# Two scan halves and one state step of the mixer, one z tile later in the plan

## The chip, the cores and the metric

The kernel runs on one core of a Trainium2 chip. The core has five engines that work beside each other, each through its own list of instructions in order: TensorE (PE, matmuls into PSUM), VectorE (DVE), ScalarE (ACT), GpSimd (POOL) and SyncE (SP, which only issues transfers). POOL issues transfers too, among them all that add to what is already in the target. An instruction waits on semaphores that other engines or landed transfers raise. The metric is device time in microseconds (us) of one execution.

## The reference

One step of a hybrid decoder trunk, all in fp32, for 512 tokens of a new sequence and 8 single new tokens of running ones (520 columns in all): `h += 0.5 ffn1(norm(h))`, `h += mixer(norm(h))`, `h += 0.5 ffn2(norm(h))`, and a last norm. The change lies in the mixer, whose input projection gives four things: `u_pool` (512 features) for a causal pooling mix, `z` (1024) as a gate, `xbc` (1536) for a convolution of four taps followed by SiLU, and `dt` (16 heads). The convolved `xbc` is split in x (1024 = 16 heads of 64), B and C (2 groups of 128 each), and goes through a scan over 4 chunks of 128 tokens:

```python
Acs = jnp.cumsum(dtc * A.reshape(G, Hg), axis=2)
decay = jnp.exp(jnp.where(mask, seg, -jnp.inf))          # seg = Acs[l] - Acs[s]
scores = jnp.einsum('bclgn,bcsgn->bclsg', Cc, Bc)
y_diag = jnp.einsum('bclsg,bclsgh,bcsgh,bcsghp->bclghp', scores, decay, dtc, xc)
states = jnp.einsum('bclgn,bclgh,bclghp->bcghpn', Bc, decay_end * dtc, xc)
# h <- exp(Acs[-1]) * h + states, chunk after chunk; y_off reads the state before its chunk
y_off = jnp.einsum('bclgn,bcghpn,bclgh->bclghp', Cc, h_prev, jnp.exp(Acs))
y = y_diag + y_off + d_skip * x
```

Then `y * silu(z)` is normed by group, joined with the pooling mix, and multiplied by `w_out`. The new states of pooling, convolution and scan are outputs too. The 8 sample tokens take one step of the same recurrence from a given state.

## The kernel before

Activations lie with features on the 128 partitions and the 520 columns along the free axis, in two halves of 260. An fp32 product is made of three matmuls (`mm3`, L122): weights and activations are split in a high and a low part (`whi`, `wlo`, `xh`, `xl`), and hi·hi (L123), hi·lo (L126) and lo·hi (L127) add up in one PSUM bank. A weight tile arrives in `raw` by SP (L119), ACT casts the high part (L107), and for the late kind ACT writes `-raw` rounded (L110) and a transfer of POOL adds the weights to it (L111), which leaves the low part.

The mixer is written as short stages, each named by a letter and a number, and two strings give their order: `CONV_PLAN`, then, after the pool `cv` of the convolution's buffers is released and `cz` is opened, `GATE_PLAN`. The letters that matter here:

- `x j`: input projection of x tile j (48 matmuls), its convolution (`U` emptied from PSUM by L781 to L783, first tap on ACT at L867, three taps on VectorE at L869) and SiLU into `X[:, j]` (L871, L872). `x7` is the last of them.
- `X1`: `sample_x(1)`, one VectorE command (`sxdt`, L965), which reads the sample columns of X tiles 4 to 7.
- `A j`: `ssd_a`, the part of the scan without the state; j runs over chunk j % 4 of group j // 4, so `A3` is the fourth chunk of group 0 and `A4` the first chunk of group 1, which reads X tiles 4 to 7. On PE two small products into `pb` (L1038, L1039) and four transpositions of X into `px` (L1046). A broadcast load fetches the decay rows `ab` from DRAM (L1048, SP). POOL, ACT and VectorE make from them `we` (L1052, L1053), `E` (L1058), `cd` (L1060) and the masked decay in `ab` itself (L1063 to L1068, L1074); from `px` come `xdt` (L1070) and `xw` (L1073), from `pb` come `bt` (L1041) and `scm` (L1043).
- `B j`: `ssd_b`, the step with the state: `yo` (L1083), `pst` (L1086), `yd` (L1089) on PE, the state `hst` (L1095 on POOL, L1096 on VectorE), and the sum into X (L1099 to L1103).
- `z j`: input projection of gate tile j (48 matmuls), emptied into `zs` by L1113.
- `s2`: two sample steps: loads of `cb` (L970) and `h` (L972) on SP, and four VectorE commands each (`junk`, L975).
- `p`, `c`, `m`: the pooling mix; `m j` is six matmuls into `pm`, emptied by L924 and L925. `e0` stores four small states (L1172 to L1175).

The strings are the order in which the program is written down. The builder then moves instructions between engines' lists by its own timeline, and chooses PSUM banks (eight, `ppm`) and buffers, so that a token's instructions may stand some places from where its neighbours are. The buffers that tie the stages are few: `ab`, `bt`, `scm` have three each, `xdt`, `xw`, `we`, `cd`, `E` have two, `cb` shares three with other small tiles, and `h0` has four. A load of `ab` can go out only when the `B` three steps earlier has read its buffer. SP issues in its list's order, so a load also stands behind every transfer ahead of it whose data isn't ready.

Of the kernel before, what the change touches and what calls it, by code (L numbers as in the profile page):

```python
# [36 lines left out]

CONV_PLAN = (
    "b0 b1 d0 b2 b3 x0 x1 v0 d1 x2 x3 d2 X0 p0 y0 c0 A0 p1 x4 m0 x5 B0 c1 p2 m1 A1 x6 c2 p3 A2 B1 x7 "
    "c3 X1 m2 A3 B2 e0"  # L40
)
GATE_PLAN = (
    "A4 z0 s2 B3 z1 s2 m3 z2 s2 B4 z3 s2 A5 z4 s2 B5 A6 z5 G0 s2 z6 A7 s2 z7 s2 B6 o0 H0 o1 B7 o2 G1 "
    "o3 g0 g1 H1 g2 g3"
)
LAST_PLAN = "h0 h2 h1 n0 h3 n1 n2 n3"
# [1252 lines left out]
```

## Time and profile before

| | us |
|---|---|
| median of 3 runs | 981.19 (973.34 to 981.55) |
| profiled execution, own time | 977.54 |
| its span, first to last instruction | 975.8 |
| PE busy | 945.4 |
| VectorE busy | 856.6 |
| ACT busy | 700.3 |
| POOL busy | 233.6 |

The profile is of one execution. Its times count from the first instruction, and its span is 1.74 us shorter than the execution's own time. A row of the timeline gives start, length, engine, line, operation, output and inputs, shape, count of merged instructions, and in brackets the idle time of that engine just before it with what ended it. PE's matmuls overlap: a 260-column matmul is listed with 0.28 us, while the next one starts 0.12 us later. So the time of a piece of PE work is read from start to start. The mixer's plan runs from some 357 to 600 us of the span.

### The profile page before, as it was taken

What the parts mean: (1) busy time and instruction counts of PE and PEld (TensorE: products, weight loads), DVE (VectorE), ACT (ScalarE), POOL (GpSimd) and SP (SyncE); (2) the same over time, 40 slices, a digit from 0 to 9 for tenths busy, and PEclk for the clock granted to TensorE, in tenths of its full rate; (3) what the DMA queues carried; (4) which work ended last, traced back from release to release, by engine and by line L of the source; (5) the groups of instructions that cost most, each with busy time, mean ns of one, the idle gap of its engine ahead of it and who ended that gap; (6) DMA issues with size and microseconds to landing.
All of it is one profiled execution on the core that took longest, in us unless ns stands there. A gap on an engine that the chain in (4) does not pass through costs nothing.

```text
span 975.8 us, 20309 instructions
## 1 busy us (share of the span) xinstructions
PE 945.4 (97%) x7636; PEld 924.0 (95%) x7636; DVE 856.6 (88%) x1610; ACT 700.3 (72%) x1287; POOL 233.6 (24%) x341
## 2 busy tenths in 40 slices
PE   7999999999999999999899999999999999999995
PEld 6999999999999999999799999899999999999995
DVE  7999899989989698688879866999989999999876
ACT  8776777777777475686676546678778788887864
POOL 0111211221121000156522111122332333333300
PEclk9999999999999999999999999999999999999998
DMA  7665766576566243264588777467687678777732
GB/s 242 167 154 136 190 149 148 126 184 180 119 152 165 66 150 118 88 205 117 148 232 225 177 173 165 119 146 179 152 220 185 167 174 222 178 159 189 191 90 89
DMA packets 66739, 157.01 MB, mean 161 GB/s; under 512 B 9608, under 2 KB 22856, under 8 KB 66640
## 3 DMA queue, kind: packets, MB, share of 16 engines
q1 hardware_dynamic: 41168, 103.78, 33.5%
q0 software_dynamic: 25472, 51.92, 29.3%
q8 instruction: 60, 0.98, 0.4%
q14 instruction: 39, 0.32, 0.1%
HBM read 148.33 MB, written 7.34 MB: 160 GB/s over the span
## 4 chain that ended last, share of the span: by engine, by line
PE 81%; DVE 7%; ACT 4%; DMA 4%; issue 2%; POOL 1%; SPq 0%; DVEq 0%; ACTq 0%; POOLq 0%
PE A L127 7%; PE A L123 7%; PE A L126 7%; PE BE L123 6%; PE BE L126 6%; PE BE L127 6%; PE P L315 3%; PE wo L123 2%; PE wo L127 2%; PE wo L126 2%; PE A1d L127 2%; PE A1d L126 2%; PE A1d L123 2%; DMA ab<-scr_acs 1%; PE A2d L127 1%
## 5 line engine op out<-in xcount | busy, mean ns | idle before, releaser
L437 ACT COPY ac<-A 128x260 f32<-128x260 f32 x123 | 45.3, 370 | 20.5 <-PE A L127 20.1
L385 DVE TENSOR_TENSOR s<-raw 128x1024 f32<-128x1024 f32 x41 | 49.9, 1217 | 2.6 <-DMA raw<-in_w2gu 2.4
L1005 POOL DMA_DIRECT2D out_nss<-hs x32 | 20.6, 643 | 84.3 <-DVE hs L1023 74.9
L123 PE MATMUL inz<-xh_mx,whi_inz 128*128 128x260 f32 x128 | 37.5, 293 | 1.0 <-DVE E L1099 1.0
L315 PE MATMUL P<-xg_f,raw 128*128 128x260 f32 x128 | 32.7, 409 | 5.4 <-DMA raw<-in_w1gu 5.4
L123 PE MATMUL wo<-catg,whi_wo 128*128 128x260 f32 x128 | 37.1, 290 | 0.0
L126 PE MATMUL inz<-xl_mx,whi_inz 128*128 128x260 f32 x128 | 36.9, 288 | 0.0
L127 PE MATMUL inz<-xh_mx,wlo_inz 128*128 128x260 f32 x128 | 36.9, 288 | 0.0
L123 PE MATMUL inx<-xh_mx,whi_inx 128*128 128x260 f32 x128 | 36.4, 285 | 0.0
L127 PE MATMUL wo<-catg,wlo_wo 128*128 128x260 f32 x128 | 36.2, 283 | 0.0
L127 PE MATMUL inx<-xh_mx,wlo_inx 128*128 128x260 f32 x128 | 36.2, 283 | 0.0
L126 PE MATMUL wo<-catg,whi_wo 128*128 128x260 f32 x128 | 36.1, 282 | 0.0
L126 PE MATMUL inx<-xl_mx,whi_inx 128*128 128x260 f32 x128 | 36.1, 282 | 0.0
L315 PEld LDWEIGHTS P<-xg_f,raw 128*128 128x128 f32 x128 | 25.7, 205 | 9.5 <-ACT xg_f L192 5.4
L449 DVE TENSOR_TENSOR tg<-BE,ac 128x520 f32<-128x520 f32 x41 | 28.4, 692 | 5.2 <-PE BE L127 5.2
L869 DVE SCALAR_TENSOR_TENSOR A<-U,h,A 128x544 f32<-128x544 f32 x36 | 28.1, 781 | 4.9 <-ACT A L867 4.6
L107 ACT CAST whi_wo<-raw_wo 128x1024 fp32r<-128x1024 f32 x12 | 12.6, 1047 | 27.0 <-issue 18.1
L1123 DVE TENSOR_TENSOR h<-wo,h 128x260 f32<-128x260 f32 x48 | 19.4, 419 | 13.7 <-PE wo L127 13.7
L458 DVE TENSOR_TENSOR tg<-tg,r_f 128x520 f32<-128x520 f32 x41 | 28.4, 693 | 1.2 <-ACT tg L456 1.0
L975 DVE SCALAR_TENSOR_TENSOR junk<-h,cb 128x128 f32<-128x128 f32 x64 | 21.5, 335 | 8.2 <-DMA cb<-scr_bc 7.3
L455 DVE TENSOR_TENSOR tg<-tg,r_f 128x520 f32<-128x520 f32 x41 | 28.4, 692 | 0.1
L386 DVE TENSOR_TENSOR s<-s,raw 128x512 f32<-128x512 f32 x41 | 28.0, 682 | 0.0
(1802 smaller groups left out, 4805.6 us busy)
## 6 DMA issues: line engine op xcount, KB each, us to landing
raw<-in_w2gu SPq DMA_DIRECT2D x44, 512.0 KB, 5.0
raw<-in_w1gu SPq DMA_DIRECT2D x42, 512.0 KB, 4.6
raw_1d<-in_w1d SPq DMA_DIRECT2D x24, 384.0 KB, 3.9
raw_2d<-in_w2d SPq DMA_DIRECT2D x24, 384.0 KB, 4.1
raw_wo<-in_w_out SPq DMA_DIRECT2D x12, 512.0 KB, 6.1
wlo_wo<-in_w_out POOLq DMA_DIRECT2D x12, 512.0 KB, 7.4
ab<-scr_acs SPq DMA_DIRECT2D x8, 512.0 KB, 5.4
h<-in_state_ssm SPq DMA_DIRECT2D x16, 256.0 KB, 6.5
```

The source lines that it names most:

```text
L123: first = nc.tensor.matmul(ps, whi, xhi, start=start, stop=False, **kw)
L126: nc.tensor.matmul(ps, whi, xlo, start=False, stop=False, **kw)
L127: nc.tensor.matmul(ps, wlo, xhi, start=False, stop=stop, **kw)
L315: nc.tensor.matmul(self.banks[f, u][b][:, :HB], ws(self.raw[f][:, u], j + 4 * q), xg[:, slot[q]], start=j == q == 0, stop=j == 3 and q == ...
L385: nc.vector.tensor_tensor(out=s1, in0=diag, in1=up0, op=ALU.add)
L386: nc.vector.tensor_tensor(out=s2[:, 0], in0=s1[:, 1], in1=raw[:, 0, :nb], op=ALU.add)
L437: nc.scalar.copy(keep, out[:, :HB])
L449: nc.vector.tensor_tensor(out=tg, in0=self.BE[k][:, :, :HB], in1=a, op=ALU.add)
L455: nc.vector.tensor_tensor(out=tg, in0=tg, in1=r, op=ALU.mult)
L458: nc.vector.tensor_tensor(out=tg, in0=tg, in1=r, op=ALU.mult)
L869: nc.vector.scalar_tensor_tensor(out=A[:, :n], in0=U[:, j : j + n], scalar=w(j), in1=A[:, :n], op0=ALU.mult, op1=ALU.add)
L975: nc.vector.scalar_tensor_tensor(out=junk, in0=h0[:, q], scalar=1.0, in1=cb, op0=ALU.mult, op1=ALU.mult, accum_out=ysm[:, 4 * g + q, b : b ...
```

## The change

In `CONV_PLAN` the token `A3` goes from between `m2` and `B2`; in `GATE_PLAN` it comes back behind `z0`. `A4` moves from ahead of `z0` to behind `z1`, and `B3` from behind `z0` and its `s2` to behind `z1` and `A4`; the first `s2` now follows `A3`, the second follows `B3`. No stage is added or removed, and no other line of the kernel differs.

```diff
 CONV_PLAN = (
     "b0 b1 d0 b2 b3 x0 x1 v0 d1 x2 x3 d2 X0 p0 y0 c0 A0 p1 x4 m0 x5 B0 c1 p2 m1 A1 x6 c2 p3 A2 B1 x7 "
-    "c3 X1 m2 A3 B2 e0"
+    "c3 X1 m2 B2 e0"
 )
 GATE_PLAN = (
-    "A4 z0 s2 B3 z1 s2 m3 z2 s2 B4 z3 s2 A5 z4 s2 B5 A6 z5 G0 s2 z6 A7 s2 z7 s2 B6 o0 H0 o1 B7 o2 G1 "
+    "z0 A3 s2 z1 A4 B3 s2 m3 z2 s2 B4 z3 s2 A5 z4 s2 B5 A6 z5 G0 s2 z6 A7 s2 z7 s2 B6 o0 H0 o1 B7 o2 G1 "
     "o3 g0 g1 H1 g2 g3"
 )
```

In the lists that the builder makes of it, PE's pieces from `m2` to `z2` stood as `A3`, `B2`, `A4` without its last transposition, `z0`, `B3`, `z1` with that last transposition inside, `m3`, `z2`. They now stand as `B2`, `z0`, `A3`, `z1`, `A4`, `B3`, `m3`, `z2`. On SP the decay rows of `A5` move from behind the store `out_ncs` to ahead of it, those of `A6` from behind `A5`'s to behind four sample loads. On ACT the SiLU of `x7` moves ahead of the `we` and the four `ab` activations of `A5`. On VectorE the taps of `x7` move ahead of the mask products (L1074) of `A3` and `A4`, and `A4`'s mask product moves behind `sxdt` and the evacuations of `z0`.

## The prediction

> **What bounds the kernel now.** I read the page first: its busy shares and its chain.
>
> ```profile
> span 975.8 us, 20309 instructions
> PE 945.4 (97%) x7636; PEld 924.0 (95%) x7636; DVE 856.6 (88%) x1610; ACT 700.3 (72%) x1287; POOL 233.6 (24%) x341
> PE 81%; DVE 7%; ACT 4%; DMA 4%; issue 2%; POOL 1%; SPq 0%; DVEq 0%; ACTq 0%; POOLq 0%
> ```
>
> TensorE (PE) is busy for 945.4 of 975.8 us and carries 81% of the chain, so the change can win only what PE loses where the plan is touched: where it stands idle, and where it works at a lower clock. The edited tokens fall between the end of `m2` and `z2`, so I cut that stretch at the events of PE's timeline and asked for the busy time of each part. The columns are the stretch, its length, busy time of PE, PEld, DVE, ACT and POOL, granted clock, DMA share and GB/s.
>
> ```profile
> 466.85:473.71 6.86, 4.74 (x42) 3.38 (x40) 5.99 (x18) 6.40 (x14) 4.51 (x10) 1.00 0.33 67
> 473.71:479.57 5.86, 5.86 (x48) 5.86 (x49) 5.47 (x14) 3.81 (x12) 1.50 (x3) 1.00 0.94 183
> 486.04:493.16 7.12, 4.85 (x29) 4.64 (x27) 4.15 (x18) 6.90 (x12) 1.91 (x3) 0.76 0.87 217
> 493.16:620.00 126.84, 126.84 (x1026) 121.71 (x1025) 100.32 (x292) 75.22 (x104) 23.71 (x27) 1.00 0.75 185
> 620.00:976.00 356.00, 339.36 (x2755) 334.20 (x2753) 325.82 (x553) 275.29 (x566) 100.83 (x143) 0.99 0.66 165
> ```
>
> PE loses 2.12 us (6.86 - 4.74) around `B2` and `A4`, and 2.27 us (7.12 - 4.85) inside `z1`, where the granted clock is 0.76 as well. From 493.16 to 620 it has no idle time at all. So what is won before 493.16 isn't swallowed by a wait in the 127 us behind it; the second FFN (16.64 us idle in 356) is the only place left to give it back. The PE timeline shows who made it wait:
>
> ```profile
> 466.85 0.27 PE L1038 MATMUL pb<-ident,BC 128*128 128x128 f32 x1
> 467.61 1.06 PE L1083 MATMUL yo<-BC,hst 128*128 128x128 f32 x8
> 470.49 0.33 PE L1038 MATMUL pb<-ident,BC 128*128 128x128 f32 x1
> 472.19 0.55 PE L1046 MATMUL px<-ident,X 128*128 128x128 f32 x3 [1.15 <-DVE xdt L1070]
> 473.71 0.39 PE L123 MATMUL inz<-xh_mx,whi_inz 128*128 128x260 f32 x1 [0.97 <-DVE E L1099]
> 479.57 1.05 PE L1083 MATMUL yo<-BC,hst 128*128 128x128 f32 x8
> 482.44 0.39 PE L123 MATMUL inz<-xh_mx,whi_inz 128*128 128x260 f32 x1
> 488.59 0.33 PE L1046 MATMUL px<-ident,X 128*128 128x128 f32 x1 [2.27 <-ACT X L871]
> 489.26 0.42 PE L123 MATMUL inz<-xh_mx,whi_inz 128*128 128x260 f32 x1
> 492.44 0.28 PE L123 MATMUL pm<-catp,wph 128*128 128x260 f32 x1
> 493.16 0.28 PE L123 MATMUL inz<-xh_mx,whi_inz 128*128 128x260 f32 x1
> 516.88 0.36 PE L123 MATMUL inz<-xh_mx,whi_inz 128*128 128x260 f32 x1
> ```
>
> From the top: A3's transpositions, `B2`, A4's transpositions (the fourth is missing), `z0`, `B3`, `z1`, the late fourth transposition, `m3`, `z2`; the last row is `z5`. The first two waits are for PSUM banks that VectorE still has to empty (`xdt` of A3, `E` of B2). The third is for the data of the last transposition: tile 7 of X, the last convolution's SiLU (call it X7).
>
> **The change, part by part.** It adds and removes no arithmetic; it moves four PE pieces. Each by its start-to-start time: A3's transpositions 467.61 - 466.85 = 0.76, A4's the same, `B2` 470.49 - 467.61 = 2.88, `z0` 479.57 - 473.71 = 5.86, `B3` 482.44 - 479.57 = 2.87, `z1` 5.86 like `z0`, `m3` 493.16 - 492.44 = 0.72. The sum is 19.71 us; the kernel before takes 493.16 - 466.85 = 26.31. So **6.60 us** are loss: 4.39 us of idle and some 2.2 us of slow matmuls, mostly behind the third wait (0.42 us each at 489.26, 0.28 elsewhere). That is the most that this edit can win.
>
> Now what it leaves. The build's order on PE becomes `m2`, `B2`, `z0`, A3's transpositions, `z1`, A4's (all four together), `B3`, `m3`, `z2`.
>
> *The two bank waits.* By that order `B2` and `z0` start in banks that were emptied earlier; A3's transpositions take those of the x7 tile and of `yo` of B2, `z1` takes those of `m2`; all are asked for after the 5.86 us of `z0`, not at once. I take both waits (1.15 + 0.97) as gone.
>
> *The wait for X7.* PE reaches the fourth transposition of A4 at 466.85 + 2.88 + 5.86 + 0.76 + 5.86 and A4's first instructions, some 0.6 (of its 0.76): 482.8. When is X7 ready? ACT's rows before:
>
> ```profile
> 479.55 0.22 ACT L1060 ACTIVATE cd<-ab 128x8 f32<-128x8 f32 x1 [2.05 <-DMA ab<-scr_acs]
> 482.01 0.21 ACT L1053 ACTIVATE we<-we 128x8 f32<-128x8 f32 x1 [2.24 <-POOL we L1052]
> 482.12 1.27 ACT L1058 ACTIVATE E<-ab 64x512 f32<-64x512 f32 x2
> 484.02 1.04 ACT L107 CAST whi_inz<-raw_inz 128x1024 fp32r<-128x1024 f32 x1
> 484.96 1.06 ACT L110 ACTIVATE wlo_inz<-raw_inz 128x1024 fp32r<-128x1024 f32 x1
> 486.61 1.28 ACT L871 ACT_TABLE_LOAD   x1
> 487.91 0.63 ACT L871 ACTIVATE X<-A 128x512 f32<-128x512 f32 x1
> ```
>
> X7 stands behind `cd` of the next chunk, which waits for that chunk's decay rows (`ab` of A5, a broadcast load on SP's queue). In the new order `we` (with its 2.24 us wait for POOL) and the four activations of `ab` stand behind X7, while `cd`, `E`, the two casts of `z3`, A3's `bt` and the table load stay ahead. The load itself:
>
> ```profile
> 471.21 0.34 SPq L1172 DMA_DIRECT2D out_ncp<-ncp  x1
> 473.06 0.34 SPq L1173 DMA_DIRECT2D out_ncs<-sconv  x1
> 473.50 9.43 SPq L1048 DMA_DIRECT2D ab<-scr_acs  x2
> DMA to landing us min/median/max: 3.5/5.4/6.8
> 483.23 0.78 DVE L869 SCALAR_TENSOR_TENSOR A<-U,h,A 128x544 f32<-128x544 f32 x1
> 488.68 0.19 DVE L965 TENSOR_TENSOR sxdt<-sdt,X 128x32 f32<-128x32 f32 x1 [2.48 <-ACT X L872]
> ```
>
> (The fourth line is the landing of all loads of `ab`.) SP is past two of these moves: A5's load now stands behind `out_ncp` and ahead of `out_ncs`. It can issue at 471.21 + 0.34 = 471.55 instead of 473.50; its buffer, read last by `B2`, is free at 466.85 + 2.88 = 469.73. With the 6.05 us that it took before (479.55 - 473.50) it lands at 477.6. Then 0.1 for `cd` (482.12 - 482.01, a command of the same size), 1.27, 0.94 (start to start), 1.06, at most `cd`'s 0.22 for the small `bt`, 1.28 and 0.63: X7 is ready at **483.1**, 0.3 us after PE asks. Bounds: landings of 3.5 and 6.8 give 480.6 and 483.9. The other input is the third tap of the convolution. It moves ahead of the mask products of A3 and A4 on VectorE; were it still at 483.23, X7 would end at 484.6 (0.7 more for the tap, 0.63 for the SiLU, the table being loaded). So the wait is 0 to 1.8 us; I take 0.3, by the row of this very load.
>
> *What is queued behind the added wait.* On VectorE `sxdt` waits for X7 (2.48 us at 488.68 before); behind it now stand the evacuations of both banks of `z0` and one of `z1`, then four commands on A5's `ab`, sample steps, and the other bank of `z1`.
>
> ```profile
> 488.78 0.76 DVE L1113 TENSOR_TENSOR zs<-inz,r_mx 128x260 f32<-128x260 f32 x2
> 493.86 0.48 DVE L1065 TENSOR_SCALAR ab<-ab,tok 128x128 f32<-128x128 f32 x2
> 497.95 0.29 DVE L975 SCALAR_TENSOR_TENSOR junk<-h,cb 128x128 f32<-128x128 f32 x1
> 479.66 2.32 POOL L1052 TENSOR_TENSOR we<-ab,tok 128x8 f32<-128x8 f32 x1 [4.44 <-DMA ab<-scr_acs]
> 495.25 1.27 ACT L1063 ACTIVATE ab<-ab,tok 128x128 f32<-128x128 f32 x4
> DMA to landing us min/median/max: 5.4/8.0/8.9
> 493.30 0.33 SPq L970 DMA_DIRECT2D cb<-scr_bc  x1
> ```
>
> (The line on landing is that of the `wlo` loads of the z tiles.) `yd` of B3, `m3` and `z2` write those banks. `yd` stands two thirds into `B3`'s 2.87 us, some 1.9 after the transpositions; `z0`'s first bank is empty some 0.6 after X7 (`sxdt`, half of 0.76): cover 1.3 us. `z2`'s first bank is the tightest, since the commands on `ab` overwrite what POOL's `we` reads, and POOL issues `wlo` of `z3` ahead of `we`. That cast is done at 481.0 by the sum above; with a microsecond for the issue `we` starts at 482 and is done by 484.3 if it takes its 2.32. Then 2 x 0.48, two steps of 0.29 and 0.4 make 1.9: the bank is free by 486.2, and `z2` wants it at 486.6. I cost it at nothing; without this cover of 0.4 it is up to 1 us. All later PE pieces keep their order, and the row 493.16:620.00 says that none waits; only the second FFN has a few VectorE and ACT instructions exchanged, which I bound at 0 to 1 us and take at 0.2.
>
> *The sum.* -6.60 + 0.3 + 0.2 = **-6.1 us**: the profiled execution took 977.54, so 971.4. The median of the runs shown is 981.19, 3.65 us above that execution; the prediction is 981.19 - 6.1 = **975.1**. The runs themselves lie between 973.34 and 981.55, so some 1% is what a measurement here tells from no change.
>
> *The clock.* Of the 6.60 us, about 2.2 hang on the low clock behind the 2.27 us wait. [...]
>
> **The rivals.**
>
> *1. X7 still decides.* If A5's load goes out no earlier than before (473.50), X7 comes at 483.1 + 1.95 = 485.05, PE waits 2.2 us, and the clock falls again (2.2): 4.4 us of the gain stay lost. 981.19 - 6.6 + 4.4 = 979.0. For it: the load's issue hangs on POOL's `ncp` through SP's order. Against: `out_ncp` was at 471.21, and it is the only one ahead.
>
> *2. Nothing comes of it.* The second FFN takes back what the mixer gains, since its 16.64 us of idle show that others decide there too: 981.2. For it: that idle time. Against: it is under 5% of that stretch, and PE's work, which sets its pace, moves forward as a whole.
>
> *3. Slower: A6's decay load is late, and `z5` with it.* That load moves behind four loads for the samples on SP (`cb` and `h`, each freed only by VectorE's sample steps), and ACT's casts for `z5` stand behind what it feeds. With the sample loads some 6 us earlier than at 493.30 and an estimate of 2.5 us for the four of them, it goes out near 490 and lands 3.5 to 6.8 later; ACT needs some 5.4 by the rows of its kinds (`cd`, `we`, `E`, four of `ab`, one exponential, two casts), and `wlo` lands 5.4 to 8.9 after that: 504.3 to 511.1. PE wants `z5` at 516.88 - 6.5 = 510.4. So by rows the price is 0 to 0.7; it beats the gain once `wlo` lands after 516.9. If the crowded queue (share 0.94 in 473.71:479.57) adds half of the sum of the longest landings (7.9), it lands at 519.0: 8.6 us lost in place of 6.5 won, and 2.2 of clock; +4.3, or 985.5.
>
> **How the numbers follow.** Forecast 0.56, rival 1 0.20, rival 2 0.12, rival 3 0.12. The range leaves out the upper tail of rival 3 and the runs that lie lowest: the forecast less the 7.85 us by which the lowest run lies under the median would be 967.3, and 985 lets in most of rival 3. Faster by over 1% (below 971.4) needs 3.7 us beyond the forecast, from the spread of runs: 0.15. Slower by over 1% (above 991) needs more than rival 3's price: 0.06. Within 1%: 0.79.
>
> **What would show it.** In the changed profile: PE without idle time over 0.5 us from `m2` to `z2`, `z2` near 486.9, granted clock 1.00 there; `cd` of A5 at 477.6 and X7 near 483.1; `sxdt` right behind it; `z5` near 510.5 with no wait for `wlo`. Wrong if ACT's `cd` still waits to 479.5, if the px transposition waits over 1 us, or if `z2` or `z5` start with an idle time.

## The result and the profile after

The changed kernel takes 986.43 us (median of 11 runs, 982.87 to 987.14); the kernel before, run beside it, 977.98 us (median of 11, 973.34 to 981.55). The ratio is 1.0078 with a 95% interval of 1.0057 to 1.0100: slower by 0.8%, inside the bound of 1%, but on the wrong side of zero, and 1.4 us above the range of the prediction. The profiled execution took 984.14 us (before: 977.54). The prediction stood on a median of three runs of the kernel before, 981.19; with eleven that median is 3.2 us lower, so the change itself costs 8.45 us.

From the page of the kernel after, the span and the busy times:

```profile
span 982.4 us, 20305 instructions
PE 945.2 (96%) x7636; PEld 924.1 (94%) x7636; DVE 857.3 (87%) x1610; ACT 700.2 (71%) x1287; POOL 229.9 (23%) x341
```

PE is busy for as long as before (945.2 against 945.4 us), so the 6.6 us of span are added idle time of PE. The windows of the kernel after, cut at events of PE (end of `m2`, `z2`, `yo` of B5, `z5`) and at 627, which answers to the 620 of the prediction, with the columns of the prediction's windows, show where:

```profile
466.31:486.02 19.71, 19.71 (x170) 17.85 (x169) 18.27 (x50) 19.11 (x39) 7.79 (x14) 1.00 0.64 148
486.02:506.11 20.09, 20.09 (x171) 19.16 (x170) 13.02 (x59) 9.57 (x20) 3.01 (x4) 1.00 0.51 128
506.11:523.96 17.85, 5.49 (x35) 4.14 (x34) 8.31 (x35) 8.56 (x10) 3.93 (x5) 0.66 0.96 243
523.96:627.00 103.04, 103.04 (x818) 99.77 (x817) 82.36 (x208) 59.18 (x80) 16.76 (x19) 0.99 0.69 166
627.00:982.40 355.40, 340.03 (x2762) 334.93 (x2760) 326.22 (x554) 275.36 (x566) 100.69 (x143) 0.99 0.66 166
```

The first row is the forecast to the digit: 19.71 us from `m2` to `z2` instead of 26.31, no idle time, clock 1.00. `z2` starts 7.14 us earlier than before (486.02, was 493.16). The third row takes it back and more. It holds B5 and A6's small products, and the same stretch of the kernel before is one row of 3.61 us:

```profile
513.27:516.88 3.61, 3.61 (x35) 2.68 (x34) 3.61 (x11) 3.60 (x8) 2.48 (x2) 1.00 1.02 240
```

17.85 - 3.61 = 14.24 us are lost there, 12.36 as idle time and the rest at a granted clock of 0.66. PE's timeline after names what it waited for:

```profile
506.11 1.05 PE L1083 MATMUL yo<-BC,hst 128*128 128x128 f32 x8
509.52 1.12 PE L1086 MATMUL pst<-xw,bt 128*128 128x512 f32 x2 [2.35 <-POOL xw L1073]
520.65 1.97 PE L1089 MATMUL yd<-ab,xdt 128*64 128x128 f32 x16 [10.01 <-DVE ab L1074]
```

`yd` of B5 waits 10.01 us for A5's mask product (L1074), a command of VectorE, and `z5` starts behind it at 523.96 without a wait of its own. VectorE's timeline after, and ACT's, follow it back:

```profile
500.34 0.29 DVE L1065 TENSOR_SCALAR ab<-ab,tok 128x128 f32<-128x128 f32 x1 [6.79 <-ACT E L1058]
519.16 0.29 DVE L975 SCALAR_TENSOR_TENSOR junk<-h,cb 128x128 f32<-128x128 f32 x1 [9.33 <-DMA cb<-scr_bc]
519.38 1.22 DVE L1074 TENSOR_TENSOR ab<-ab,scm 128x1024 f32<-128x1024 f32 x1
```

```profile
476.53 0.22 ACT L1060 ACTIVATE cd<-ab 128x8 f32<-128x8 f32 x1
481.43 0.63 ACT L871 ACTIVATE X<-A 128x512 f32<-128x512 f32 x1
499.23 0.22 ACT L1060 ACTIVATE cd<-ab 128x8 f32<-128x8 f32 x1 [10.40 <-DMA ab<-scr_acs]
```

VectorE stands twice: 6.79 us for what ACT makes of A6's decay rows (ACT waits 10.40 us for their load), and 9.33 us for `cb` of sample step 7; the mask product is the next command behind that. Both are loads. Here are their issues, from the timelines of SP and POOL after:

```profile
485.98 0.33 SPq L970 DMA_DIRECT2D cb<-scr_bc  x1
486.35 0.42 SPq L972 DMA_DIRECT2D h<-in_state_ssm  x1
489.02 0.42 SPq L972 DMA_DIRECT2D h<-in_state_ssm  x1
489.54 0.39 SPq L1048 DMA_DIRECT2D ab<-scr_acs  x1
501.47 0.33 SPq L970 DMA_DIRECT2D cb<-scr_bc  x1
504.65 0.81 SPq L119 DMA_DIRECT2D raw_wo<-in_w_out  x2
505.55 0.78 SPq L970 DMA_DIRECT2D cb<-scr_bc  x1
```

```profile
488.24 0.88 POOL L111 DMA_DIRECT2D wlo_inz<-in_w_in  x1 [0.23 <-ACT bt L1041]
504.92 0.89 POOL L111 DMA_DIRECT2D wlo_inz<-in_w_in  x1 [5.43 <-ACT wlo_inz L110]
```

A6's load goes out at 489.54, behind four sample loads (before: the second load of the row at 473.50, out by 482.93 and ahead of all of them). While VectorE stands, the sample steps don't run and no sample load goes out from 489.54 to 501.47; then the held ones go out within a few us of each other, together with A7's decay rows and two weight loads, and `cb` of step 7 is the row at 505.55. The view of the DMAs gives the time from issue to landing as its last column. First the issues of 485.9 to 486.8, then those of 488.2 to 490, then those of 504.6 to 505.7:

```profile
h<-in_state_ssm SPq DMA_DIRECT2D x1, 256.0 KB, 3.4
cb<-scr_bc SPq DMA_DIRECT2D x1, 64.0 KB, 3.0
...
wlo_inz<-in_w_in POOLq DMA_DIRECT2D x1, 512.0 KB, 9.3
ab<-scr_acs SPq DMA_DIRECT2D x1, 512.0 KB, 9.6
h<-in_state_ssm SPq DMA_DIRECT2D x1, 256.0 KB, 8.9
...
raw_wo<-in_w_out SPq DMA_DIRECT2D x2, 512.0 KB, 11.2
wlo_inz<-in_w_in POOLq DMA_DIRECT2D x1, 512.0 KB, 11.5
cb<-scr_bc SPq DMA_DIRECT2D x1, 64.0 KB, 13.5
```

A `cb` of 64 KB lands in 3.0 us or in 13.5. The loads that SP issued 0.8 and 1.3 us behind POOL's accumulating transfer of 488.24 landed with it or just after it (497.5; 497.9 and 499.1); those issued 1.9 and 2.3 us ahead of it were quick.

### The profile page after: what moved, and what is told of

It is laid out like the page before. It is cut to its first block, busy times and chain, and to the rows that moved or that the text cites. A ratio compares the mean times of both kernels' runs of the same rounds, so it can differ in the third digit from the quotient of the medians.

```text
span 982.4 us, 20305 instructions
## 1 busy us (share of the span) xinstructions
PE 945.2 (96%) x7636; PEld 924.1 (94%) x7636; DVE 857.3 (87%) x1610; ACT 700.2 (71%) x1287; POOL 229.9 (23%) x341
## 4 chain that ended last, share of the span: by engine, by line
PE 80%; DVE 9%; ACT 5%; DMA 3%; issue 2%; POOL 0%; SPq 0%; DVEq 0%; ACTq 0%; POOLq 0%
PE A L127 7%; PE A L123 7%; PE A L126 7%; PE BE L123 6%; PE BE L126 6%; PE BE L127 6%; PE P L315 3%; PE wo L123 2%; PE wo L127 2%; PE wo L126 2%; PE A2d L127 2%; PE A2d L126 2%; PE A2d L123 2%; PE A1d L127 2%; PE A1d L126 2%
```

## The experiments

The theories at the start: A, the late load of A6 stops VectorE, the stopped sample steps delay their own loads, and A5's mask product stands behind the last of these; B, the moved A4 and B3 themselves make B5's inputs late; C, the transfers are too many for the stretch in any order. Ratios are against the kernel before in the same series of runs, with 95% intervals; the changed kernel has 1.0078 (1.0057 to 1.0100).

### 1. A6's load ahead of the sample loads

A stage `L j` holds the allocation and load of `A j` (`L5`, `L6` stand around `B3`), and the sample loads `cb` of steps 3 and 4 and `h` of steps 4 and 5 are held behind `L6`'s. Shown are the lines for `cb`; those for `h` are alike.

```diff
+        with tc.issue_after(ld[2, 1].ins) if (b, g) >= (3, 0) and g == 0 and b < 6 else nullcontext():
             nc.sync.dma_start(out=cb, in_=rows_bc(b, 1, g))
```

> The changed kernel, with one thing altered: on SP's list the load of A6's decay rows (ab) stands ahead of the sample loads cb of step 3, h of step 4, cb of step 4 and h of step 5, instead of behind them; the lists of the four other engines stay the same. Theory A (the late load stops VectorE, the stopped sample steps delay their own next loads, and A5's mask product stands behind the last of those): the load goes out at about 485.5 instead of 489.5, lands in about 4 to 5 us, ACT's cd no longer waits 10.4 us, VectorE does not stop 6.8 us on E, PE has no wait of 10.0 us at yd (L1089) and none of 2.4 us at pst (L1086); the time falls by the 12.4 us of idle and some 2 us of clock, to 970 to 974, or 4 to 8 us under the kernel before. Rival B (the moved A4 and B3 themselves make B5's inputs late): 984 to 987, as changed. Rival C (the transfers crowd each other wherever the load stands): the load still takes 8 us or more to land and about half is won, 978 to 981.

Measured: 1.0009 (0.9985 to 1.0032); 979.05 us beside 977.99. Of the 0.78% that the changed kernel loses, 0.69 are gone, so the late load is the root of the loss, and B falls. But the time of the kernel before is only reached. (The profiled execution took 974.78 us, the shortest of the twelve, so its trace may show less waiting than the median has.) In its DMA view, A6's load (issued 486.47) and `cb` of step 7 (issued 500.90, behind A7's load and two of `raw_wo`) have:

```profile
ab<-scr_acs SPq DMA_DIRECT2D x1, 512.0 KB, 4.8
...
cb<-scr_bc SPq DMA_DIRECT2D x1, 64.0 KB, 9.1
```

The first link of A is mended (4.8 us instead of 9.6), the second not: PE still waits 2.42 us at `yd` of B5 for L1074, and its clock is 0.83 in the next 10 us. I expected 970 to 974, which counted the second link as a mere consequence of the first.

### 2. The mask product ahead of the sample steps

```diff
-    "... m3 z2 s2 B4 z3 s2 A5 z4 s2 B5 A6 z5 ..."
+    "... m3 z2 s2 B4 z3 A5 s2 z4 s2 B5 A6 z5 ..."
```

> The changed kernel with the token A5 ahead of its neighbour s2 in the plan. SP's list stays the same in the stretch, so the load of A6's decay rows is as late as in the changed kernel; on VectorE A5's xdt (L1070), scm and mask product (L1074) now stand ahead of nearly all steps of samples 6 and 7. Theory A (the last link is the mask product that stands behind sample step 7): the load lands late as before (near 499), VectorE still stops some 6.8 us on E, but PE's wait of 10.0 us for L1074 at yd and the 2.4 us for xw shrink to 0 to 3 us together; time 974 to 979. Rival A2 (the late load reaches PE by another way, by ACT's casts for z5 or by A6 itself, and the sample steps are bystanders): 984 to 987.

Measured: 1.0071 (1.0040 to 1.0102); nothing gained. The link itself is shown: no wait for L1074 is left. From the list of PE's waits in the mixer, the three longest:

```profile
PE inz L127 <- DMA wlo_inz<-in_w_in: 3.6, 1, 3.6
PE psr_y L170 <- DVE E L1099: 2.1, 1, 2.1
PE pst L1086 <- POOL xw L1073: 1.6, 1, 1.6
```

The late load then reaches PE by ACT's casts and `wlo` of `z5` (3.6 us, the path of the prediction's rival 3), and the sample steps, now later on VectorE, keep the PSUM bank that the gate's norm (`psr_y`) needs. The time is that of rival A2, its reason is half of each: freeing the last victim doesn't help while the cause is there.

### 3. and 4. A4 alone late; A4 and B3 late, A3 where it was

```diff
-    "A4 z0 s2 B3 z1 s2 m3 ...        (before)
+    "z0 s2 B3 z1 A4 s2 m3 ...        (3)
+    "z0 s2 z1 A4 B3 s2 m3 ...        (4)
```

> The kernel before with A4 alone moved behind z1; A3 and B3 stay. On SP the load of A6's decay rows stays ahead of all sample loads, as in the kernel before. Theory A: the wait for X7 (2.27 us) and the slow clock behind it (about 2.2) go, as A4 is asked for after z1, and so does the bank wait of 1.15 us; nothing stops at B5: 4 to 6 us under the kernel before, so better than both. Rival B (A4 late is what hurts B5, since its B4, xdt and bank turns come later): slower than before by 3 us or more, with PE waiting between z4 and z5.

> The kernel before with A4 and B3 moved as in the change; A3 stays in the convolution's plan. On SP the load of A6's decay rows then stands behind two sample loads (cb of step 3, h of step 4) instead of four. Theory A: the load goes out near 487, ahead of wlo of the next z tile, and lands by 492 to 494; VectorE stops for it at most 1 us; no wait over 1 us at B5; 3 to 6 us under the kernel before. Rival B (B3 one z tile later is what delays A6 and B5): the wait at B5 is there as in the changed kernel, 6 us or more slower than before. Rival C (landing is slow wherever the load stands among sample loads): 0 to 5 us slower than before.

Measured: 1.0027 (1.0001 to 1.0054) and 1.0056 (1.0030 to 1.0082). Both expectations missed. From the lists of PE's waits, the two longest each, (3) and then (4):

```profile
PE wo L123 <- DVE hst L1096: 4.9, 1, 4.9
PE px L1046 <- ACT X L871: 2.1, 1, 2.1
...
PE px L1046 <- ACT X L871: 3.4, 1, 3.4
PE wo L127 <- DMA wlo_wo<-in_w_out: 2.9, 1, 2.9
```

With A3 still in the convolution's plan the wait for X7 stays. A5's load then goes out at 473.01 (3) and 473.56 (4), behind `out_ncs`, and ACT's `cd` waits 4.59 and 2.44 us for it; in the changed kernel it goes out at 471.24. So it is A3's move that brings X7 forward, and the place of A5's load fits as the way, as the prediction had it. And in both a wait of 3 to 5 us appears at the beginning of the output projection, in (3) behind sample loads that took up to 15.6 us, in (4) for `wlo` beside sample loads of up to 12.5 us. So A4 alone, and A4 with B3, are each enough to bunch the loads somewhere; A3 and B3 alone weren't run.

### 5. and 6. The second place on SP's list

In the kernel before, `cb` of step 7 and `h` of step 8 stand ahead of A7's load and of `raw_wo`. (5) restores that on top of 1, (6) on the changed kernel alone.

```diff
+        with tc.issue_after(ld["h", 0, 1].ins) if (c, g) == (3, 1) else nullcontext():
             ... nc.sync.dma_start(out=ab, in_=scr_acs[...])
+        with tc.issue_after(ld["h", 0, 1].ins) if j == 0 and d2 < 2 else nullcontext():
             wh, wl = load_unit(ins["w_out"][j, d2], 1024, f"wo{j}{d2}", True)
```

> As e1_load_first (A6's decay load first), and beside it cb of sample step 7 and h of step 8 stand ahead of A7's decay load and of the two weight loads raw_wo on SP's list, as they do in the kernel before; behind that the lists of VectorE and ACT differ in a few places only. In e1_load_first cb of step 7 was issued at 500.90 behind those three big loads, VectorE waited 4.73 us for it, and PE 2.42 us for the mask product behind it, with a granted clock of 0.83 in the next 10 us. Theory A (the place of the loads on SP's list is all there is to the loss): cb of step 7 lands within 7 us of its issue and by 506, PE has no wait over 0.5 us at yd of B5, and 2.4 us of idle and 1.7 us of clock come back: 974 to 976 median, 3 to 4 us under the kernel before. Rival C (the transfers of that stretch crowd each other in any order): the wait at yd or another of 2 to 4 us (wlo of z5, raw_wo) stays, 978 to 981.

> The changed kernel with only the second of the two places mended: cb of sample step 7 and h of step 8 ahead of A7's decay load and of the two loads raw_wo. A6's decay load is as late as in the changed kernel. Theory A: VectorE still stops some 6.8 us near 493 to 500 and the sample loads are issued from 501 on as before, but cb of step 7 goes out near 504 instead of 505.55 and lands in 6 to 8 us instead of 13.5; PE's wait of 10.0 us at yd falls to 2 to 5 us: 977 to 982. Rival A2 (the stop for A6's load alone decides): no gain, 984 to 987.

Measured: 1.0001 (0.9976 to 1.0026) and 1.0060 (1.0035 to 1.0086). In (5) B5 is clean, PE has no idle time from 460 to 530, and the wait has moved on; from PE's waits, VectorE's timeline and the DMA view (the `cb` issued at 528.46, with a transfer of POOL 0.64 us ahead of it; the profiled execution, 981.39 us, is the longest of the twelve, whose median is 977.04):

```profile
PE psr_y L170 <- DVE E L1108: 5.8, 1, 5.8
...
541.81 0.29 DVE L979 SCALAR_TENSOR_TENSOR junk<-h,cb 128x128 f32<-128x128 f32 x1 [7.80 <-DMA cb<-scr_bc]
...
wlo_wo<-in_w_out POOLq DMA_DIRECT2D x1, 512.0 KB, 10.4
cb<-scr_bc SPq DMA_DIRECT2D x1, 64.0 KB, 13.2
```

In (6) the stop for A6's load remains, and PE waits 2.4 us for `xw`, 2.7 for L1074 and 3.9 at the gate's norm: the wait at `yd` fell as A expected, the time (983.97) didn't. The places on the list are not all there is (in (5) A forecast 3 to 4 us under the kernel before, and 0.7 came): the next sample load that meets a bunch hands its lateness on.

### 7. and 8. Both kernels without the sample steps

```diff
+    nc.vector.memset(ysm, 0.0)
+
     def samples(n):
-        for _ in range(n):
-            if smp:
-                sample(*smp.pop(0))
+        return
```

> The changed kernel without the 16 sample steps: their loads of cb and h and their four VectorE commands each are left out (the sample tokens' scan term is then zero). To be read against e8_before_no_samples. Theory A: with no sample loads on SP the load of A6's decay rows goes out by 486 and nothing stops at B5, so the gain of the change shows: 5 to 7 us faster than e8_before_no_samples. Rival B (the moved A4 and B3 themselves make B5 late): 5 us or more slower than e8_before_no_samples. Rival D (the first wait, for X7, was itself due to the sample loads): no difference.

> The kernel before without the 16 sample steps, left out in the same way. Theory A: the waits of 1.15, 0.97 and 2.27 us from m2 to z2 stay, nothing else changes on PE's path: 0 to 5 us under the kernel before. Rival D: the wait for X7 goes, and the time falls by 5 us or more.

Measured: 971.18 us after and 975.61 us before, the change now worth 4.43 us in medians (5.6 us in the profiled spans, 968.3 and 973.9), where 5 to 7 were expected. With no sample step in VectorE's list nothing stops at B5, and the change is faster. It is less than 6.6, and there is less to win: without sample steps the kernel before waits 0.75 us for X7, not 2.27.

### 9. Without the sample states' bytes

All `h` loads (4 MB) are left out, one tile of zeros stands for them; `cb` loads and steps stay.

```diff
+    hzero = mp.tile([P, 4, P], F32, tag="h0", bufs=4, name="hzero")
+    nc.vector.memset(hzero, 0.0)
 ...
-        h0 = mp.tile([P, 4, P], F32, tag="h0", bufs=4, name=f"h0_{b}{g}")
-        nc.sync.dma_start(out=h0, in_=ins["state_ssm"][:, b, 4 * g : 4 * g + 4])
+        h0 = hzero
```

> The changed kernel with the sample steps' state loads (h, 16 loads of 256 KB on SP) left out: every step multiplies by one tile of zeros; the small loads of cb and all VectorE commands stay (the sample tokens' scan term and what follows from it are then wrong). A6's decay load still stands behind two loads of cb on SP's list. Theory A in its first form (the order of the waits on SP's list does it): A6's load is still held until VectorE has run the steps that free cb, goes out near 489, and part of the loss at B5 stays: 977 to 983. Theory C (the transfers are too many for the stretch, and order only decides whom it hits): with 4 MB less to move every load lands within 6 us, nothing waits over 1 us from z2 to the output projection, and the gain shows: 970 to 974.

Measured: 1.0038 (1.0012 to 1.0064), 981.73 beside 979.39: about half of the loss is gone, but not what C expected. In the trace, which is of the longest of the ten executions (987.82 us), PE still waits 7.9 us for L1074, and A6's load, 0.8 us behind a transfer of POOL, is as slow as ever with 4 MB less to move:

```profile
wlo_inz<-in_w_in POOLq DMA_DIRECT2D x1, 512.0 KB, 9.5
ab<-scr_acs SPq DMA_DIRECT2D x1, 512.0 KB, 9.4
```

So it isn't the bytes of the samples that make this load slow. That made theory W: a load that goes out behind POOL's accumulating transfer lands only with it.

### 10. and 11. Spread, and all steps later

(10) is 5 with the last four `s2` further back; (11) is the changed kernel with every `s2` one place later.

```diff
-    "... A5 z4 s2 B5 A6 z5 G0 s2 z6 A7 s2 z7 s2 B6 o0 H0 o1 B7 ...      (changed kernel)
+    "... A5 z4 B5 A6 z5 G0 s2 z6 A7 z7 s2 B6 o0 s2 H0 o1 s2 B7 ...      (10)
-    "z0 A3 s2 z1 A4 B3 s2 ... A7 s2 z7 s2 B6 o0 ...                     (changed kernel)
+    "z0 A3 z1 A4 B3 s2 ... A7 s2 z7 s2 B6 s2 o0 ...                     (11)
```

> As e5_both_places (both places on SP's list mended), and the last four of the eight s2 of the plan spread further back: the fifth behind G0, the sixth behind z7, the seventh and eighth in the output projection behind o0 and o1. In e5_both_places PE waited 5.8 us at psr_y for E of B6, because VectorE stood 7.80 us before a cb whose load was in a stretch with DMA share 1.04. Theory C (the transfers of 500 to 545 are too many there; spread out, they hurt no one): that wait goes, no other over 1 us comes from z2 to the end of the mixer, 971 to 974, better than the kernel before by 4 to 7 us. Rival E (any sample step in VectorE's in-order list finds its load late and hands the wait on): another wait of 3 us or more appears in the output projection or at the gate of group 1, 976 to 981.

> The changed kernel with each s2 one place later in the plan and nothing else (no order forced). On SP's list A6's decay load then stands ahead of all sample loads, but A7's and two raw_wo stand ahead of cb of step 5. Theory A with C: no stop at A6, the wait at B5 falls below 4 us, but a sample load that lands late hands a wait to PE further back: 975 to 981. If the plan alone cures it: 971 to 974. Rival B: 984 or more.

Measured: (10) 0.9931 (0.9905 to 0.9957), 971.42 us beside 979.39: **better than both kernels**, 0.7% under the kernel before, as C expected. How much of that is the change's own isn't shown, since the spread was not run on the kernel before. PE doesn't stand anywhere in the mixer behind `m2`:

```profile
480.00:530.00 50.00, 50.00 (x425) 47.21 (x425) 44.17 (x159) 36.10 (x61) 14.35 (x17) 1.00 0.80 212
530.00:560.00 30.00, 30.00 (x251) 28.02 (x251) 26.56 (x90) 16.05 (x18) 5.66 (x6) 1.00 0.81 210
560.00:620.00 60.00, 60.00 (x452) 58.24 (x452) 45.50 (x85) 38.72 (x52) 8.30 (x10) 1.00 0.64 147
```

(11) 0.9994 (0.9970 to 1.0018): A6's load goes out in time, but `cb` of step 7 meets A7's and `raw_wo`, and a wait of 5.3 us for L1074 remains, where less than 4 was expected.

### 12. and 13. POOL's transfers left out

`wlo` of z4 (12), or of z4 to z7 (13), isn't loaded, the low part of those weights being zero; SP's list is that of the changed kernel.

```diff
-            nc.scalar.activation(out=lo[:, q:], in_=src[:, q:], func=AF.Copy, scale=-1.0)
-            nc.gpsimd.dma_start(out=lo[:, q:], in_=late, accum_op=ALU.add)
+            nc.scalar.activation(out=lo[:, q:], in_=src[:, q:], func=AF.Copy, scale=0.0 if name in ("inz4",) else -1.0)
+            if name not in ("inz4",):
+                nc.gpsimd.dma_start(out=lo[:, q:], in_=late, accum_op=ALU.add)
```

> The changed kernel with one transfer left out: POOL's accumulating load of the low weight part (wlo) of the gate tile z4, whose low part is then zero (so z4 loses the lo-hi product's value, while the matmuls still run). Nothing else is changed; on SP's list A6's decay load still stands behind four sample loads. In the changed kernel that transfer was issued at 488.24 and landed 9.3 us later, and the loads that SP issued behind it, h of step 5 at 489.02 and A6's ab at 489.54, landed 8.9 and 9.6 us later, about when it did; the two loads that SP issued shortly ahead of it landed in 3.0 and 3.4 us. Theory W (a load that goes out behind POOL's accumulating transfer lands only with it): ab is issued near 489.5 as before but lands within 5 us, VectorE does not stop 6.8 us on E, and what is left is as in e1_load_first: 977 to 981. Theory A alone (the place behind the sample loads costs the time, whatever POOL does): ab lands after 8 us or more, 984 to 987.

> The changed kernel with the same transfer left out for the gate tiles z4 to z7 (their low parts are zero, the matmuls still run). Theory W: the loads of cb between 500 and 515 land within 7 us too, PE has no wait over 1 us from z2 to the output projection, and the whole gain of the change shows: 970 to 974. If the share of the queues by SP's own loads is what counts: cb of step 7 still takes over 8 us, a wait of 2 us or more stays, 976 to 981.

Measured: 1.0028 (1.0002 to 1.0054) and 1.0007 (0.9976 to 1.0038). The DMA views: `ab` of A6 and `h` of step 5 in (12), issued at 489.97 and 489.45; then `cb` of step 7 in (12), issued at 502.12; then the same `cb` in (13), issued at 501.80:

```profile
ab<-scr_acs SPq DMA_DIRECT2D x1, 512.0 KB, 5.7
h<-in_state_ssm SPq DMA_DIRECT2D x1, 256.0 KB, 3.5
...
wlo_inz<-in_w_in POOLq DMA_DIRECT2D x1, 512.0 KB, 10.7
cb<-scr_bc SPq DMA_DIRECT2D x1, 64.0 KB, 13.0
...
cb<-scr_bc SPq DMA_DIRECT2D x1, 64.0 KB, 7.3
```

With that one transfer gone, the same two loads at the same place of the list take 5.7 and 3.5 us instead of 9.6 and 8.9: W holds for them. `cb` of step 7 falls from 13.5 to 7.3 once its neighbours are gone too.

What held them back? In the changed kernel both loads were out by 489.93, and the 16 DMA engines were busy for only 0.34 of 489 to 492, so at first it wasn't that they were full. The DMA view of 492.5 to 494.5 counts packets by queue; `q0 software_dynamic` is POOL's queue (it is missing in the same stretch of (12), where POOL's transfer is left out), `q1 hardware_dynamic` is SP's:

```profile
q0 software_dynamic: 93, 0.38, 94.3%
q1 hardware_dynamic: 40, 0.04, 6.2%
```

From 494.5 to 498, with POOL's transfer nearly done, SP's queue moved 0.74 MB, which is nearly all of the two loads. So the bytes themselves came late, not only the signal of their landing; why SP's queue stood back isn't shown.

A fast landing is only part of the cure. In (12) VectorE stops 2.93 us for A6 instead of 6.79, but the sample loads still go out in a bunch behind that stop, `cb` of step 7 takes 13.0 us, and PE waits 8.3 us for L1074 at B5, where 2.4 as in experiment 1 was expected. Of the changed kernel's 0.78%, 0.50 come back in (12) and 0.71 in (13). (13) was expected at 970 to 974 by W and took 979.02, inside the range of the other theory, that SP's own loads crowd each other (though that one had `cb` at over 8 us): waits of 2.6 us at B5 and of 2.4 us at the gate's norm stay, the second beside `wlo` of the output weights, which (13) leaves in.

### 14. The spread alone

The plan of 10 without any forced order of loads.

> The changed kernel with the last four s2 of the plan spread further back as in e10_spread, but with no order forced on SP: A6's decay load stands behind four sample loads and goes out behind the accumulating transfer of z4. Theory W with A: the load lands 9 us after its issue, VectorE stops some 6.8 us, and PE waits 5 us or more at B5: 979 to 985. If spreading the steps alone cures it: 970 to 974.

Measured: 1.0072 (1.0042 to 1.0101), 985.44 us. A6's load took 9.8 us, PE waited 9.8 us for L1074 and 2.5 for `xw`. The better version needs both, the place of the loads and the spread.

## Why the prediction was wrong

- **The gain: right.** 6.60 us from `m2` to `z2` were forecast at -6.60 + 0.3; 6.60 came (19.71 for 26.31). Both bank waits went. `cd` of A5 ran at 476.53 (forecast 477.6) and X7 was ready at 482.06 (forecast 483.1), so the wait of 0.3 was none; `sxdt` and the banks of `z0` to `z2` cost nothing.
- **The low clock: right.** 1.00 where it was 0.76; in the stretch of the new stall of 12.36 us it was 0.66.
- **The step that failed:** "All later PE pieces keep their order, and the row 493.16:620.00 says that none waits". The row says that with the old order of loads nobody waited; the change moved A6's load on SP's list, and the row couldn't speak for that. The price was 14.24 us at B5 (experiment 1 traces most of it to the place of that load: 2.42 us of waiting are left of 12.36).
- **Rival 3 had the cause and the wrong victim.** It named A6's load and its issue near 490 (489.54), and its time, 985.5, is the nearest to 986.43. The nearness is in part luck: 3.2 us of it come from the base of 981.19, and the loss was 8.45 us where it had 4.3. By its rows, a landing of 3.5 to 6.8, the price was 0 to 0.7, and only an assumed crowding made it more; the landing took 9.6. And it followed the load along ACT to `wlo` of `z5`, while the sample steps on VectorE carried it to B5, ahead of `z5`; the path by `z5` is real, too, but comes second (3.6 us in experiment 2). Its chance of 0.12 was too small: it was the only rival that followed the moved DMA past its queue.
- **The second FFN: small, as forecast, but the other way.** It was bounded at 0 to 1 us of loss. PE's idle time in the last window is 15.37 us (355.40 - 340.03); before it was 16.64, of which 0.2 lie behind the end of the span. So it gave back about 1 us.
- **What the landing hung on.** The prediction bounded it by the spread of earlier rows of `ab`, 3.5 to 6.8 us. It hung on the transfer of POOL ahead of it: 9.6 us behind that transfer, 5.7 without it (experiment 12), and the packets show the load's own bytes late.

What stays open: why SP's queue stands back behind POOL's transfer, and how the last 2 to 6 us would fall out in another run of loads. The kernels of experiments 1, 5, 11 and 13 lose them at different places (B5, the gate's norm), and no run separates the number of bytes there from their order. Each trace is of one execution, and those of 1 and 5 lie 4 us on either side of their medians.

## What to carry to other kernels

When an edit moves a load on a queue, price the load by what stands ahead of it on every queue (A6's took 9.6 us behind POOL's transfer, 5.7 without it), not by the spread of its old landings (3.5 to 6.8), and ask which in-order list has a command that waits for it: what stands behind that command pays (here PE, with 10.01 us at `yd` of B5). A stretch without idle time is covered only for the order of loads that it was measured with; a few us gained ahead of it can bring loads together that used to pass each other (`cb` of step 7 landed in 5.1 us before the change and in 13.5 after it).

## What the runs showed of the hardware

A load issued on SP's queue behind an accumulating transfer of POOL's queue landed with that transfer or later: 8.9 and 9.6 us for 256 and 512 KB at 0.8 and 1.3 us behind it, 3.5 and 5.7 us with the transfer left out. Just ahead of it 64 and 256 KB took 3.0 and 3.4 us. With 4 MB of other loads taken away the 512 KB still took 9.4 us. The distance matters: in the kernel before, A5's load went out 0.42 us behind POOL's transfer and landed 1.8 us ahead of it (479.52 and 481.31); in experiment 3 it went out 0.52 us behind and landed with it (481.25 and 481.09). In the mixer (340 to 620 us) of all sixteen traces, counting loads with a traced landing, nine of eleven that were issued 0.25 to 0.5 us behind such a transfer landed ahead of it, and one of 123 that were issued 0.5 to 3 us behind. With two such transfers 4.5 us apart, 64 KB took 13.5 us, and 7.3 in experiment 13, without both.

The granted clock also fell without a wait above 1.16 us: without the sample steps the kernel before had the same two bank waits (1.16 and 0.97 us, 1.5 us apart) and right behind them a clock of 0.50 for 3.41 us (474.96 to 478.37), where the kernel before with them had 1.00 from 470 to 480. So this pair of waits cost, by an estimate from those 3.41 us at half the clock, some 1.7 us more than its idle time in the one kernel's trace, and no clock in the other's.
